# A hybrid retention and sliding-window layer on one core: the opening update of retention put into its first step, and the order of all engines planned with other numbers

## The chip, the core and the metric

The kernel runs on one core of one Trainium2 chip. The time is that of one execution on the device, in microseconds (us). Three runs of the kernel before took 667.78, 668.63 and 671.33 us; the median, 668.63 us, is the time before. A profiled execution leaves a trace with the start and duration of each instruction on the matmul engine (PE, with its weight loads shown apart as PEld), the vector engine (DVE), the scalar engine (ACT), POOL and the queue of SP, which issues the DMAs.

## The reference, cut to what matters

```python
h = rms_norm(x, norm_w)                       # (1, 2048, 1024)
proj = einsum('bsd,de->bse', h, w_in)         # 1024 -> 2816 columns
rq, rk, rv, rg, sq, sk, sv, sg = split(proj, offsets)
rq, rk = rotary(rq), rotary(rk)               # 4 heads of 64
ro = retention(rq, rk, rv)                    # chunks of 128 tokens, values of 128 a head
ro = group_norm_per_head(ro) * ret_norm_w * silu(rg)
so = sliding_window_attention(rms(sq), rms(sk), sv, sinks, rel_bias) * silu(sg)
out = x + concat(ro, so) @ w_out              # 1024 -> 1024
```

In retention each of 16 chunks has four parts: an update of the state (its keys against its values), scores (queries against keys, times a decay mask), a cross part (queries against the state of the chunks before) and an output part (scores against values).

## The kernel before

**Products.** The projections are made in four large products: the window's columns (W2, 512 wide), retention's queries, keys and first values (W1, 384), the gates (W3, 512) and the output (W4, 512). Each is a fast matrix product of seven smaller products over eight pairs of chunks, and each small product is 12 matmuls: four blocks of the inner dimension by three passes (high by high, high by low, low by high, written `acc<-w,x`). DVE and ACT split every operand into its high and low part and add the results up. The order on PE is W2, then W1, then W3, then W4.

**Other work on PE.** Between the small products stand the window's logits (`m<-ks,qT`, 64 matmuls for a pair of chunks, each of two passes in the trace), its values (`m<-pT,vn`, 72 for a pair), single transposes of keys (`m<-ident,kn`), transposes of gated retention outputs (`m<-ident,ro` or `m<-ident,go`, four for a chunk), and retention's steps. These use parts of the array (32 or 64 rows or columns) and not the whole, and each is one operation of the planner with many instructions.

**Retention's steps.** The loop at the end of `retention` makes one PE operation for each step from -1 to 8: the cross part of the pair of chunks before (`m<-state,qkT`), the update of the pair after (`m<-v,qk`), the scores of this pair (`m<-qkT`) and the outputs of the pair before (`m<-v,sT`). Each part takes 16 matmuls. Step -1 holds only the update of pair 0, in two banks of PSUM; step 0 holds the update of pair 1 and the scores of pair 0. Inside a step `mark`, two tiny copies on DVE, keeps the cross part and the outputs in order. After a step ACT moves the outputs out (`ro`), DVE takes their statistics (`st`), masks the scores (`sT`) and adds up the states (`state`).

**What sets the order.** Nothing runs in the order in which the code names it. `op` records each operation with a cost and a due time, and `Program.emit` plans them greedily: at each turn it takes the operation that can start first, and of those the one with the earliest due time. `SHIFT` moves the due times by label, `SHARE` limits how many buffers a use may hold, `AHEAD` and `AHEAD_OF` how far ahead of PE loads and splits may go. `WIN`, `RET` and `GATE` are the first due time and the distance of the chunks of the window, of retention and of the gates, counted in small products; `LEAD` says how early a gate must be ready. On PE a change between whole-array and partial-array matmuls is charged, and `LATER`, `CROWD`, `MOST` and `SOONER` gather such operations.

**Instruction blocks.** `emit` also counts PE's instructions (`many`, times `MORE` = 1.0125 for what is added later): a block border stands at `FIRST` = 193 and every `PIECE` = 256 after it, a block is taken to be asked for `ASKED` instructions ahead of its border and to take `LONG` us, and an operation that would come to a border sooner is planned later.

**Where results wait.** `HELD` lists results that stay in SBUF and are not stored and loaded again: sums of x for the products W1 and W3, retention's outputs (`ro`), the window's queries (`q`) and outputs (`so`), and gates. `TURNED` lists what is transposed through a store and a transposing DMA; what is not in it is transposed on PE. `EARLIER_Q`, `EARLIER_K` and `SCALED` set how early the queries and keys go on that way.

Of the kernel before, what the change touches and what calls it, by code (L numbers as in the profile page):

```python
# [39 lines left out]
P = 128  # L40
NCH = S // P
NP = NCH // 2
# [21 lines left out]
SHARE = {"x": 56, "raw": 221, "acc": 63, "wr": 28, "wh": 18, "att": 23, "ret": 40, "rin": 186, "gate": 29, "mix": 89, "norm": 17, "res": 29, "turned": 11, "vn": 3, "first": 5, "block": 3, "rest": 6}  # L64

AHEAD_OF = {"x": 5.5, "wh": 15.5}

AHEAD, SPARE, SPARED = 11.0, 4, ("raw", "wr")

# [25 lines left out]

PIECE, FIRST, ASKED, LONG, MORE = 256, 193, 320, 5.5, 1.0125  # L100

LATER, CROWD, MOST, SOONER = -3.75, 7.25, 41, -388.0
SETTLED, INSIDE = 0.8, 0.3


# [230 lines left out]

LOG = None  # L340

SHIFT = {"base": -3.5, "load xk": 0.5, "add s": 1, "load g": 3.75, "add t": -5.0, "silu": -1, "add res": -1.25, "square x": -2.5, "load phases": -0.25, "store so": -1.0, "decay": 0.5, "scale v": 1.25, "turn weights": -0.75, "no values": -0.5, "sink": -3.25, "hi w": 0.5, "load wr": 1.0, "load aq": -0.25, "qn": 0.25, "step": -0.5, "load akv": 0.25, "store r": -0.75, "store x": 1.5, "apart": 0.5, "sum so": 1.25, "load gp": -3.5, "copy s": -0.75, "sum x": 1.0, "load dec": 0.25, "store res": -0.75, "exp sink": 0.75, "store c": 0.25, "turn k": -1.5, "load vn": 0.75, "ro": -0.75, "turn by dma": -1.25, "load nw_sb": 0.5, "load go": 0.75, "ks": -1.25, "gate": -0.25, "kn": -0.5, "copy c": 0.75, "add r": -0.75, "scale w": 1.25, "rotary sum": -0.75, "factors": -0.5, "state": -0.25, "so": -1.25, "sum qk": -1.0, "load ": 0.25, "mixed": 0.75, "load snk": 0.25, "store ": -1.25, "rotary": 1, "more": 3.25, "bias": 1.25, "denominator": -0.75, "normalise": -1.25, "load wq": -0.25, "no keys": -1, "square qk": -1, "turn gated": -0.5, "load tri": -1, "exp": -1.25, "load bias": 0.25, "store s": -0.5, "logits": -1, "sum go": -1, "values": -0.5, "stats": 1.5}

TURN = (1.9635, 2.7, 1.35)


HELD = {"sums": ((3, 2), (3, 6), (3, 7), (5, 0), (5, 1), (5, 2), (5, 5), (6, 1), (6, 3), (6, 4), (6, 6)), "ro": (1, 2, 6, 10, 11, 13, 15), "q": (1, 3, 9, 12, 13), "gates": (), "so": (13,)}

TURNED = {"q": range(NCH), "qk": range(NCH), "gated": (3, 7, 14)}
EARLIER_Q, EARLIER_K = 5.5, 10.0
SCALED = (-25.0, 4.45)


def dve(n, two=False, lat=0.08):
# [24 lines left out]
def f32(n, count):  # L382
    t = count * (n / 600 + 0.01)
    return {"T": (t, t + 0.25, False)}
# [43 lines left out]
def layer(ctx, tc, xt, xfirst, xtok, nw, w_in, w_rn, qkw, sinks, biasg, rope, decays, dmask, gpow, w_out, out):  # L428
# [33 lines left out]
    def ps(share="rest", name="m"):  # L462
        return Buf("bank", None, F32, name, share)
# [60 lines left out]
    dec = fixed([P, 2, BASED, RH], "dec")  # L524
    factors = [fixed([P, NCH, RH], f"factors{i}") for i in range(2)]
# [178 lines left out]
    sums = {}  # L704
# [50 lines left out]
    turn = Buf(name="turn", ap=())  # L755
# [154 lines left out]
    def retention(at):  # L910
# [16 lines left out]
        for c in range(NCH):  # L927
            due = at(c)
            a, v = kb("a", "rin"), kb("v", "rin")
# [5 lines left out]
            if c % NP == 0:  # L935
                phases = kb("phases", "rin")
# [42 lines left out]
            else:  # L979

                def go(e, pt=pt, qk=qk):
# [6 lines left out]
                   label="qkT")  # L988
# [4 lines left out]
        norm = {}  # L993
# [28 lines left out]
        def update(c, pkv):  # L1022

            _, qk, _, v, v0, v1 = chunks[c]

            def go(e):
                for pr in range(2):
                    for i in range(2):
                        for b in range(2 if c < NCH - 1 else 1):
                            h, r, o = 2 * pr + i, halves[b], c % 2 * 256 + pr * P  # L1030
                            e.matmul(
                                pkv[b]()[halves[i], o : o + P], qk()[r, 256 + h * 64 : 256 + (h + 1) * 64],
                                v()[r, h * P : (h + 1) * P], start=True, stop=True,
                            )

            return go, [qk, v0, v1], [v]
# [48 lines left out]

            return go, [*sTs, v0, v1], [v]

        for step in range(-1, NP + 1):
            due = at(2 * step + 1)
            pair = lambda p: (2 * p, 2 * p + 1)  # L1090

            parts, writes, also, n, done = [], [], [], 0, None
            if step > 0:
                pros, begun, mark = [ps(), ps()], set(), sb("mark", [P, 2])

                def ordered(e, mark=mark, pros=pros):
                    for i in range(2):
                        V.tensor_copy(mark()[:, i : i + 1], pros[i]()[:, 256:257])

                writes += pros  # L1100
                parts += [cross(c, pros, ready[c], begun) for c in pair(step - 1)] + [(ordered, [], [mark])]
                n += 4
            if step < NP - 1:
                pkv = [ps(), ps()]
                writes += pkv
                parts += [update(c, pkv) for c in pair(step + 1)]
                n += 4
            if 0 <= step < NP:
                pss, sT = [ps(), ps()], sb("sT", [P, 512])
                writes += pss  # L1110
                also.append(sT)
                parts += [scores(c, pss) for c in pair(step)]
                n += 2.4
            if step > 0:
                parts += [outputs(c, pros, inside[0]) for c in pair(step - 1)]
                also.append(inside[1])
                n += 4

            def go(e, parts=parts):
                for part in parts:  # L1120
# [10 lines left out]
            if 0 <= step < NP:  # L1131
# [11 lines left out]
            if step < NP - 1:  # L1143
                for c in pair(step + 1):
# [477 lines left out]

WIN = (58.5, 4.0)
RET = (126.0, 2.25)
GATE = (138.5, 6.65)

LEAD = 14.0


_SHAPES = {
# [92 lines left out]
```

## Time and profile before

| | |
|---|---|
| median of three runs | 668.63 us (667.78 to 671.33) |
| the profiled execution | 672.41 us, of which 670.6 us from its first to its last instruction |
| instructions | 16293 |
| work on PE | 5960 matmuls and 5960 weight loads |
| mean granted PE clock | 0.997 |
| HBM | 96.79 MB read, 49.09 MB written |

All rows carry line L424, that of the helper that records each instruction, so operations are told apart by their tiles. A matmul of float32 operands runs in two passes and shows as two in the trace. In the rows of idle time, "issue" is time in which an engine waited for nothing that the profile shows.

### The profile page before, as it was taken

The numbers are of one execution on the slowest core, as the hardware profiler recorded it, in microseconds if no ns is written. First come the engines' busy times: TensorE is split into PE (matmuls) and PEld (weight loads), VectorE is DVE, ScalarE is ACT, GpSimd is POOL, SyncE is SP. The second block draws the span as 40 slices with busy tenths as digits, with TensorE's granted clock in tenths as the row PEclk, the third lists the DMA queues.
The fourth block names the chain that finished last, engine by engine and source line by source line (L and its number), as shares of the span: only waits on it lengthen the run. The fifth ranks groups of instructions, "written<-read, shape, count | busy, mean of one in ns | idle before, by whom it ended". The sixth has DMA issues, their size and how long they took to land.

```text
span 670.6 us, 16293 instructions
## 1 busy us (share of the span) xinstructions
PE 660.4 (98%) x5960; PEld 564.8 (84%) x5960; DVE 590.5 (88%) x1372; ACT 470.7 (70%) x1149; POOL 15.1 (2%) x39
## 2 busy tenths in 40 slices
PE   9999999999989999899999999999999999999998
PEld 7888888889979999899888888878888888888886
DVE  5999969778897998799999999979699999998762
ACT  6673897658689876596988989788999736344200
POOL 0000000023200000000000000000000000000000
PEclk9999999999989999999999999999999999999999
DMA  9965897879886978799999989898999894536222
GB/s 323 367 215 185 276 340 257 285 236 289 275 199 177 307 229 258 250 312 305 301 246 267 272 225 283 198 275 245 279 273 224 240 222 143 169 111 216 99 94 95
DMA packets 150688, 160.33 MB, mean 239 GB/s; under 512 B 64592, under 2 KB 92112, under 8 KB 150608
## 3 DMA queue, kind: packets, MB, share of 16 engines
q1 hardware_dynamic: 150464, 159.29, 80.6%
q8 instruction: 47, 0.77, 0.5%
q14 instruction: 33, 0.27, 0.2%
q10 hardware_dynamic: 144, 0.00, 0.0%
HBM read 96.79 MB, written 49.09 MB: 218 GB/s over the span
## 4 chain that ended last, share of the span: by engine, by line
PE 96%; DVE 2%; issue 1%; ACT 1%; DMA 0%; SPq 0%; ACTq 0%; DVEq 0%
PE acc L424 85%; PE m L424 11%; DVE st L424 0%; DMA v<-rq_dram 0%; ACT qk L424 0%; DVE t L424 0%; DVE x L424 0%; DVE r L424 0%; ACT apart L424 0%; DVE w L424 0%; ACT g L424 0%; DVE qk L424 0%; ACT w L424 0%; DVE mark L424 0%; DVE sT L424 0%
## 5 line engine op out<-in xcount | busy, mean ns | idle before, releaser
L424 PE MATMUL acc<-w,x 128*128 128x512 f32 (+1 forms) x2700 | 589.8, 378 | 2.3 <-issue 2.3
L424 PEld LDWEIGHTS acc<-w,x 128*128 128x128 f32 x2700 | 494.5, 189 | 86.1 <-issue 7.0
L424 DVE TENSOR_TENSOR x<-x 128x512 fp32r<-128x512 f32 (+2 forms) x220 | 143.2, 675 | 13.1 <-ACT x L424 11.2
L424 ACT ACTIVATE x<-x 128x512 fp32r<-128x512 f32 (+1 forms) x187 | 111.1, 619 | 25.9 <-PE acc L424 10.4
L424 DVE TENSOR_TENSOR w<-w 128x512 fp32r<-128x512 f32 (+3 forms) x96 | 60.5, 653 | 1.5 <-ACT w L424 1.5
L424 ACT ACTIVATE lg<-lg,nm 128x160 f32<-128x160 f32 x128 | 53.0, 418 | 6.2 <-DVE nm L424 6.1
L424 DVE TENSOR_TENSOR s<-acc,s 128x512 f32<-128x512 f32 (+1 forms) x64 | 41.6, 650 | 17.4 <-PE acc L424 17.0
L424 DVE SCALAR_TENSOR_TENSOR w<-w,nw_sb 128x512 fp32r<-128x512 f32 (+3 forms) x72 | 49.2, 706 | 1.7 <-ACT w L424 1.5
L424 ACT ACTIVATE w<-w 128x512 fp32r<-128x512 f32 (+1 forms) x72 | 41.4, 601 | 13.0 <-DVE w L424 5.8
L424 DVE CUSTOM_DVE_ANT_0 lg<-m,bias,nsnk 128x160 f32<-128x160 f32 x128 | 40.4, 375 | 3.6 <-PE m L424 3.6
L424 DVE TENSOR_TENSOR t<-acc,t 128x512 f32<-128x512 f32 (+2 forms) x33 | 21.1, 638 | 17.9 <-PE acc L424 17.5
L424 ACT ACTIVATE x<-go 128x512 fp32r<-128x512 f32 x31 | 19.2, 627 | 16.2 <-DVE x L424 5.4
L424 ACT ACTIVATE w<-w,nw_sb 128x512 fp32r<-128x512 f32 (+3 forms) x42 | 27.1, 678 | 4.0 <-DMA w<-in_w_in 2.3
L424 ACT ACTIVATE s<-acc 128x512 f32<-128x512 f32 (+1 forms) x32 | 18.1, 568 | 15.2 <-PE acc L424 14.9
L424 DVE STREAM_TRANSPOSE pT<-lg 128x640 f32<-128x640 f32 x32 | 26.0, 825 | 0.6 <-ACT lg L424 0.6
L424 DVE TENSOR_TENSOR r<-acc,t 128x512 f32<-128x512 f32 (+1 forms) x32 | 20.9, 652 | 5.9 <-PE acc L424 5.5
L424 ACT ACTIVATE qk<-qk,factors 128x64 f32<-128x64 f32 x64 | 17.0, 339 | 12.6 <-DVE mdif L424 7.0
L424 ACT ACTIVATE ro<-ro,nmu,rg 128x128 f32<-128x128 f32 x64 | 25.3, 482 | 0.3 <-DVE nmu L424 0.2
L424 ACT ACTIVATION_READ_ACCUMULATOR lg<-lg,nm 128x1 f32 x128 | 24.2, 189 | 0.0
L424 DVE TENSOR_TENSOR t<-acc,s 128x512 f32<-128x512 f32 (+1 forms) x32 | 20.7, 648 | 3.7 <-PE acc L424 2.8
L424 PE MATMUL m<-ks,qT 64*32 64x160 f32 x1024 | 20.1, 298 | 2.8 <-issue 2.8
L424 ACT ACTIVATE ro<-m 64x256 f32<-64x256 f32 (+2 forms) x55 | 22.1, 402 | 0.6
(140 smaller groups left out, 578.5 us busy)
## 6 DMA issues: line engine op xcount, KB each, us to landing
x<-in_xt SPq DMA_DIRECT2D x80, 256.0 KB, 4.7
planes_dram<-apart SPq DMA_DIRECT2D x51, 256.0 KB, 3.8
x<-s_dram SPq DMA_DIRECT2D x42, 256.0 KB, 4.2
w<-in_w_in SPq DMA_DIRECT2D x40, 256.0 KB, 5.3
xk<-in_xtok SPq DMA_DIRECT2D x32, 256.0 KB, 4.5
res<-in_xtok SPq DMA_DIRECT2D x32, 256.0 KB, 3.7
s_dram<-x SPq DMA_DIRECT2D x21, 256.0 KB, 3.9
w<-in_w_out SPq DMA_DIRECT2D x20, 256.0 KB, 4.5
```

The costliest lines, as they stand in the source:

```text
L424: return lambda *a, **k: self.order.put(op(*a, **k))
```

## The change

Retention's step -1 is gone. Step 0 now makes the updates of pair 0 and of pair 1, into four banks (two a pair), with the scores of pair 0. `many`, the planner's count of instructions, is 17 higher for a step. `TURNED` has four gated chunks (1, 8, 12, 14) in place of three (3, 7, 14). All other edits are numbers of the planner: shares, due times, distances, and what is held: seven sums in place of eleven, eight `ro` in place of seven, three `so` in place of one, one gate in place of none, and five `q` as before.

```diff
-SHARE = {"x": 56, "raw": 221, "acc": 63, "wr": 28, "wh": 18, "att": 23, "ret": 40, "rin": 186, "gate": 29, "mix": 89, ...
-AHEAD_OF = {"x": 5.5, "wh": 15.5}
-AHEAD, SPARE, SPARED = 11.0, 4, ("raw", "wr")
+SHARE = {"x": 24, "raw": 192, "acc": 88, "wr": 63, "wh": 56, "att": 56, "ret": 50, "rin": 279, "gate": 77, "mix": 93, ...
+AHEAD_OF = {"x": 8.0, "wh": 9.5}
+AHEAD, SPARE, SPARED = 24.5, 2, ("raw", "wr")
...
-PIECE, FIRST, ASKED, LONG, MORE = 256, 193, 320, 5.5, 1.0125
+PIECE, FIRST, ASKED, LONG, MORE = 256, 193, 300, 5.0, 1.0125
...
-LATER, CROWD, MOST, SOONER = -3.75, 7.25, 41, -388.0
+LATER, CROWD, MOST, SOONER = -2.0, 0.75, 35, -928.0
...
-HELD = {"sums": ((3, 2), (3, 6), (3, 7), (5, 0), (5, 1), (5, 2), (5, 5), (6, 1), (6, 3), (6, 4), (6, 6)), "ro": (1, 2, 6, 10, 11, 13, 15), "q": (1, 3, 9, 12, 13), "gates": (), "so": (13,)}
+HELD = {"sums": ((3, 2), (3, 5), (3, 6), (5, 2), (5, 7), (6, 2), (6, 5)), "ro": (0, 4, 5, 6, 7, 8, 12, 15), "q": (0, 5, 11, 13, 14), "gates": (3,), "so": (1, 12, 15)}
...
-TURNED = {"q": range(NCH), "qk": range(NCH), "gated": (3, 7, 14)}
-EARLIER_Q, EARLIER_K = 5.5, 10.0
-SCALED = (-25.0, 4.45)
+TURNED = {"q": range(NCH), "qk": range(NCH), "gated": (1, 8, 12, 14)}
+EARLIER_Q, EARLIER_K = 2.0, 6.5
+SCALED = (-30.5, 5.15)
...
-        for step in range(-1, NP + 1):
+        for step in range(NP + 1):
...
-            if step < NP - 1:
-                pkv = [ps(), ps()]
+            pkvs = {p: [ps(), ps()] for p in ((0, 1) if step == 0 else (step + 1,)) if p < NP}
+            for p, pkv in pkvs.items():
                 writes += pkv
-                parts += [update(c, pkv) for c in pair(step + 1)]
+                parts += [update(c, pkv) for c in pair(p)]
                 n += 4
...
-                f32(P, 0.935 * n), go, reads, writes, due + 0.4, "quarters", label="step", also=also, many=int(16 * n),
+                f32(P, 0.935 * n), go, reads, writes, due + 0.4, "quarters", label="step", also=also, many=int(16 * n) + 17,
...
-WIN = (58.5, 4.0)
-RET = (126.0, 2.25)
-GATE = (138.5, 6.65)
-LEAD = 14.0
+WIN = (56.5, 3.9)
+RET = (120.5, 1.45)
+GATE = (143.5, 4.5)
+LEAD = 15.5
```

How the order moves, at three places. Rows that follow each other and are alike are counted as one (x12).

On PE, the opening of retention, before, from the first update to step 0:

```order
L424 MATMUL acc<-w,x 128x512 x3
L424 MATMUL m<-v,qk 64x128 x16
L424 MATMUL acc<-w,x 128x512 x21
L424 MATMUL m<-ident,kn 128x128
L424 MATMUL acc<-w,x 128x512 x21
L424 MATMUL m<-ks,qT 32x160 x64
L424 MATMUL acc<-w,x 128x512 x42
L424 MATMUL m<-v,qk 64x128 x16
L424 MATMUL m<-qkT 64x64 x16
```

and now, with the step that follows:

```order
L424 MATMUL acc<-w,x 128x512 x33
L424 MATMUL m<-v,qk 64x128 x32
L424 MATMUL m<-qkT 64x64 x16
L424 MATMUL acc<-w,x 128x512 x51
L424 MATMUL m<-state,qkT 64x128 x12
L424 MATMUL m<-v,qk 64x128 x16
L424 MATMUL m<-qkT 64x64 x16
L424 MATMUL m<-v,sT 64x128 x16
L424 MATMUL acc<-w,x 128x512 x33
```

The visit with the first 16 updates is gone, and its matmuls stand in the next one.

On PE, in the window's part, before, one place at which values and logits stand close:

```order
L424 MATMUL m<-pT,vn 64x128 x32
L424 MATMUL m<-pT,vn 64x256 x8
L424 MATMUL m<-pT,vn 64x128 x32
L424 MATMUL m<-ident,kn 128x128
L424 MATMUL acc<-w,x 128x384 x18
L424 MATMUL m<-ks,qT 32x160 x64
L424 MATMUL acc<-w,x 128x384 x48
```

and now the closest place:

```order
L424 MATMUL m<-pT,vn 64x128 x32
L424 MATMUL m<-pT,vn 64x256 x8
L424 MATMUL m<-pT,vn 64x128 x32
L424 MATMUL acc<-w,x 128x384 x18
L424 MATMUL m<-ks,qT 32x160 x64
L424 MATMUL acc<-w,x 128x384 x21
L424 MATMUL m<-pT,vn 64x128 x32
L424 MATMUL m<-pT,vn 64x256 x8
L424 MATMUL m<-pT,vn 64x128 x32
L424 MATMUL acc<-w,x 128x384 x48
```

A second set of values now follows the logits after 21 products, where 48 stood before.

On PE, the last two steps of retention, before:

```order
L424 MATMUL acc<-w,x 128x512 x42
L424 MATMUL m<-state,qkT 64x128 x16
L424 MATMUL m<-qkT 64x64 x16
L424 MATMUL m<-v,sT 64x128 x16
L424 MATMUL acc<-w,x 128x512 x36
L424 MATMUL m<-ident,go 128x128 x4
L424 MATMUL acc<-w,x 128x512 x24
L424 MATMUL m<-state,qkT 64x128 x16
L424 MATMUL m<-v,sT 64x128 x16
L424 MATMUL m<-ident,ro 128x128 x4
```

and now:

```order
L424 MATMUL acc<-w,x 128x512 x21
L424 MATMUL m<-state,qkT 64x128 x16
L424 MATMUL m<-qkT 64x64 x16
L424 MATMUL m<-v,sT 64x128 x16
L424 MATMUL acc<-w,x 128x512 x9
L424 MATMUL m<-state,qkT 64x128 x16
L424 MATMUL m<-v,sT 64x128 x16
L424 MATMUL acc<-w,x 128x512 x45
L424 MATMUL m<-ident,ro 128x128 x4
```

The steps stand closer: between the last two are 9 products in place of 60, and between the steps ahead of them 51, 33, 27, 36, 27, 48 and 21. The transposes of gated outputs, which stood between the steps and far into W4, now all come after the last step and before W4's first product.

More of the change, by code (lines that the diff above doesn't have):

```diff
@@ L62 @@
 SMALL, COUNTS = 3, {"ms": 1, "rxt": 1, "rqk0t": 1, "rqk1t": 1, "state": 10, "sT": 2}
-SHARE = {"x": 56, "raw": 221, "acc": 63, "wr": 28, "wh": 18, "att": 23, "ret": 40, "rin": 186, "gate": 29, "mix": 89, "norm": 17, "res": 29, "turned": 11, "vn": 3, "first": 5, "block": 3, "rest": 6}
-AHEAD_OF = {"x": 5.5, "wh": 15.5}
-AHEAD, SPARE, SPARED = 11.0, 4, ("raw", "wr")
+SHARE = {"x": 24, "raw": 192, "acc": 88, "wr": 63, "wh": 56, "att": 56, "ret": 50, "rin": 279, "gate": 77, "mix": 93, "norm": 17, "res": 24, "turned": 22, "vn": 3, "first": 5, "block": 3, "rest": 6}
+AHEAD_OF = {"x": 8.0, "wh": 9.5}
+AHEAD, SPARE, SPARED = 24.5, 2, ("raw", "wr")
 STEPS = ((1, 2), (6,), (5,), (7, 4), (3,))
@@ L340 @@
 LOG = None
-SHIFT = {"base": -3.5, "load xk": 0.5, "add s": 1, "load g": 3.75, "add t": -5.0, "silu": -1, "add res": -1.25, "square x": -2.5, "load phases": -0.25, "store so": -1.0, "decay": 0.5, "scale v": 1.25, "turn weights": -0.75, "no values": -0.5, "sink": -3.25, "hi w": 0.5, "load wr": 1.0, "load aq": -0.25, "qn": 0.25, "step": -0.5, "load akv": 0.25, "store r": -0.75, "store x": 1.5, "apart": 0.5, "sum so": 1.25, "load gp": -3.5, "copy s": -0.75, "sum x": 1.0, "load dec": 0.25, "store res": -0.75, "exp sink": 0.75, "store c": 0.25, "turn k": -1.5, "load vn": 0.75, "ro": -0.75, "turn by dma": -1.25, "load nw_sb": 0.5, "load go": 0.75, "ks": -1.25, "gate": -0.25, "kn": -0.5, "copy c": 0.75, "add r": -0.75, "scale w": 1.25, "rotary sum": -0.75, "factors": -0.5, "state": -0.25, "so": -1.25, "sum qk": -1.0, "load ": 0.25, "mixed": 0.75, "load snk": 0.25, "store ": -1.25, "rotary": 1, "more": 3.25, "bias": 1.25, "denominator": -0.75, "normalise": -1.25, "load wq": -0.25, "no keys": -1, "square qk": -1, "turn gated": -0.5, "load tri": -1, "exp": -1.25, "load bias": 0.25, "store s": -0.5, "logits": -1, "sum go": -1, "values": -0.5, "stats": 1.5}
+SHIFT = {"square qk": -2.5, "load g": 3.0, "silu": -3.75, "hi w": 1.0, "no values": -2.0, "decay": -2.0, "store ro": 7.5, "copy s": -4.25, "exp sink": 7.0, "denominator": 4.25, "qn": 1.0, "turn k": -8.0, "load ": 2.25, "lo w": 0.5, "store ": -8.0, "sum w": -1.0, "load vn": 2.5, "step": -6.5, "sink": -1.25, "load w": 0.25, "turn weights": -7.0, "scale v": -0.25, "more": 4.0, "no keys": -4.5, "group norm": 1.5, "add res": 9.0, "sum x": 0.25, "gate": -1.25, "load go": -4.5, "rotary sum": -0.25, "load k4": -2.0, "load bias": 4.25, "normalise": 5.5, "store res": 8.75, "so": 4.75, "sum go": 3.75, "base": -5.5, "load aq": -8.75, "store s": 1.5, "store t": -6.5, "store x": -2.25, "load xk": -0.75, "kn": 1.25, "load akv": -0.75, "sum so": -1.5, "state": -4.0, "values": -5.5, "load dec": 3.5, "copy c": 3.0, "add s": -1.0, "rotary": -0.75, "load phases": -1.5, "stats": 2.0, "add t": -0.25, "ks": -2.0, "store apart": -0.5, "logits": -0.5, "lo x": 0.25, "load gp": 0.25, "load res": 2.0, "square x": 2.0, "load nw_sb": 3.75, "add r": -1.75, "bias": -2.75, "turn by dma": 0.25, "mixed": -1.0, "scale w": 3.75, "store r": 1.5, "exp": -2.5, "sum ro": 0.5, "turn gated": 0.5, "load wr": -1.25, "store c": 0.25, "load snk": 1.25, "load tri": -0.75, "store so": -0.5, "scale k": -0.5, "load wq": -1}
@@ L1102, in retention @@
                 n += 4
-            if step < NP - 1:
-                pkv = [ps(), ps()]
+            pkvs = {p: [ps(), ps()] for p in ((0, 1) if step == 0 else (step + 1,)) if p < NP}
+            for p, pkv in pkvs.items():
                 writes += pkv
-                parts += [update(c, pkv) for c in pair(step + 1)]
+                parts += [update(c, pkv) for c in pair(p)]
                 n += 4
-            if 0 <= step < NP:
+            if step < NP:
                 pss, sT = [ps(), ps()], sb("sT", [P, 512])
@@ L1130, in retention @@
                     evacuate(c, pros, due)
-            if 0 <= step < NP:
+            if step < NP:
                 sTs = [Part(sT, lambda t, i=i: t[:, i * 256 : (i + 1) * 256]) for i in range(2)]
@@ L1142, in retention @@
                 inside = (sTs, sT)
-            if step < NP - 1:
-                for c in pair(step + 1):
+            for p, pkv in pkvs.items():
+                for c in pair(p):
                     states = [state]
```

## The prediction

> **What bounds the kernel now.** I read the page's share of engines first, then PE's waits, then the stretches around those waits, then PE's timeline and the DMA queues there.
>
> ```profile
> span 670.6 us, 16293 instructions
> PE 660.4 (98%) x5960; PEld 564.8 (84%) x5960; DVE 590.5 (88%) x1372; ACT 470.7 (70%) x1149; POOL 15.1 (2%) x39
> PE m L424 <- issue: 2.8, 2, 2.2
> PE acc L424 <- issue: 2.3, 1, 2.3
> PE m L424 <- DVE none L424: 1.2, 1, 1.2
> PE m L424 <- DVE sT L424: 0.3, 1, 0.3
> PE m L424 <- DVE mark L424: 0.3, 1, 0.3
> 194.00:198.00 4.00, 1.81 (x89) 1.23 (x75) 3.87 (x17) 4.00 (x10) 0.00 (x0) 0.97 1.22 204
> 198.00:208.00 10.00, 10.00 (x50) 9.96 (x51) 6.29 (x26) 6.22 (x29) 0.00 (x0) 0.84 0.82 226
> ```
>
> PE is the bound: it is busy 98% of the span, and all its waits together are 6.9 us. Only 0.6 us of them are for another engine's work once the kernel runs; 5.1 us (2.8 + 2.3) are "issue", where no semaphore was late. After the first of these the granted clock (third number from the right) is 0.97 for 4 us and 0.84 for 10 us, a loss of 4 x 0.03 + 10 x 0.16 = 1.7 us. So 7.4 us can be won from waits and clock (5.1 + 1.7 + 0.6), and the rest is matmul work that the change hardly touches. The largest gain is therefore near 1.1%, while there is no such limit on the other side.
>
> What are the issue waits? Three stretches from the start to each wait count PE's matmuls before it:
>
> ```profile
> 0.00:195.05 195.05, 193.87 (x1235) 164.85 (x1236) 165.87 (x330) 139.53 (x327) 15.07 (x39) 1.00 0.83 273
> 0.00:222.75 222.75, 219.37 (x1614) 188.95 (x1614) 189.80 (x398) 160.77 (x391) 15.07 (x39) 0.99 0.83 266
> 0.00:268.85 268.85, 264.86 (x2373) 231.81 (x2373) 230.69 (x526) 196.15 (x513) 15.07 (x39) 0.99 0.85 264
> q8 instruction: 47, 0.77, 0.5%
> ```
>
> Two instructions a matmul (with its weight load), times the planner's 1.0125, give 2501, 3268 and 4805. Less 193 that is 9.02, 12.01 and 18.02 times 256: each wait stands on a block border. The last row is the page's queue of instruction fetches: 47 packets of 0.77 MB / 47 = 16 KB, and 5960 x 2 x 1.0125 / 256 = 47 blocks. PE waits for its own instructions. The third wait on the timeline and in the queues:
>
> ```profile
> 260.00 2.54 PE L424 MATMUL m<-pT,vn 32*64 32x128 f32 x144
> 262.47 1.84 PE L424 MATMUL acc<-w,x 128*128 128x384 f32 x9
> ...
> 264.17 1.81 PE L424 MATMUL acc<-w,x 128*128 128x384 f32 x9
> 265.91 2.43 PE L424 MATMUL m<-ks,qT 64*32 64x160 f32 x128
> 268.27 0.62 PE L424 MATMUL acc<-w,x 128*128 128x384 f32 x2
> 271.16 6.71 PE L424 MATMUL acc<-w,x 128*128 128x384 f32 x37 [2.27 <-issue]
> q8 instruction: 1, 0.02, 36.2%
> q1 hardware_dynamic: 1619, 1.40, 65.5%
> q8 instruction: 1, 0.02, 39.1%
> ```
>
> The three queue rows are of the stretches 260.8 to 261.1, 262.0 to 268.6 (no instruction packet at all) and 268.65 to 268.8 us. One fetch starts at 260.8 to 261.1, the next only at 268.65, as PE already stands, and PE goes on at 271.16, about 10.2 us after the first. Values (288 instructions in 2.47 us) and logits (256 in 2.36 us) eat a block each; 18 products between them are too few to cover a fetch.
>
> A rule of the Trainium skill speaks against this reading: "Runtime: NRT & Kernel Launch", Instruction fetch mechanics, says that blocks of 16 KiB (256 instructions) are fetched while the one before runs, and that the cost of a border is mostly hidden. The block's size agrees with the 16 KB above; that it is hidden does not, at these three borders of 47. It is the third rival below.
>
> **The change part by part.**
>
> *The joined update.* One visit of PE to partial-array work goes, the 16 matmuls of the order (32 in the trace) stay:
>
> ```profile
> 331.42 0.97 PE L424 MATMUL acc<-w,x 128*128 128x512 f32 x3
> 332.32 1.10 PE L424 MATMUL m<-v,qk 64*64 64x128 f32 x32
> 333.35 5.06 PE L424 MATMUL acc<-w,x 128*128 128x512 f32 x21
> 378.48 1.05 PE L424 MATMUL m<-v,qk 64*64 64x128 f32 x32
> 379.35 0.64 PE L424 MATMUL m<-qkT 64*64 64x64 f32 x32
> 421.67 0.44 PE m L424 x4
> 525.17 34.73 PE acc L424 x153
> ```
>
> From 331.42 to 333.35 are 1.93 us. Three products are 0.68 (34.73 / 153 = 0.227 each) and 32 update matmuls inside a step are 379.35 - 378.48 = 0.87, so the visit cost 1.93 - 0.68 - 0.87 = 0.38 us. That goes: **-0.4**. Four banks and two for scores make six, what any middle step holds, and 51 products (11.6 us) follow before the next step asks for banks; if that cover fails, products wait for the eight `state` adds.
>
> *A fourth gated chunk turned by DMA.* Four transposes less on PE, 0.44 us by the row of x4: **-0.4**. It adds a copy on ACT (70% busy), a store and a transposing DMA.
>
> *What is held.* Four sums less are four stores and eight loads more (W1 and W3 both read them); one `ro`, two `so` and one gate more held save eight. With the turned chunk, SP issues six transfers more, 1.5 MB of 160 MB. They hide behind queues that carry 239 GB/s on average with no row of PE waiting for a DMA; uncovered they would be 1.5 MB / 239 GB/s = 6.4 us, shared by all that wait.
>
> *The new order and the blocks.* I walk PE's new order with the durations above (values 2.47, logits 2.36, a product 0.174 or 0.227, a change of array about 0.2), counting instructions as for the waits, and take the time for two blocks, since the waits came where two in a row were short. In the order before this gives, below 10.6 us: 7.7 (the first wait, 2.19), 7.7 (the third, 2.27), and 10.0, 10.5, 10.5, 10.5, of which one waited 0.61 and three not at all. The wait is thus about 9.9 us less the span. The new order has 9.1, 9.1, 7.9, 8.1 and 10.3. The 7.9 is the triple values, 18 products, logits, 21 products, values; the 8.1 overlaps it by a block, so that a wait of 2.0 in the one lengthens the other to 10.1. The waits become 0.8 + 0.8 + 2.0 + 0 + 0.3 = 3.9 in place of 5.1: **-1.2**. Bounds: 0, if blocks come as early as at most borders, and 7.2 by counting places alone (three spacings of 21 products or less in place of two, 2.2 each, and 0.6). I take 3.9, since it follows the borders.
>
> *The clock.* Of two waits of 2.2 us, one was followed by a low clock and one not. With one such wait left I take half of 1.7: **-0.85** (bounds -1.7 and +1.7). The Trainium skill ("TensorE: Matmul & The Clock Gate", What's actually happening) has the clock fall after an idle window of about 3.4 us that runs free of the kernel. A wait of 2.19 us did it here. By that page no wait of 2 us would, and the sum would be 0.85 lower.
>
> *PE's waits for DVE.* 0.6 us now; the steps move closer together, so these may move too: **-0.3**, between -0.6 and what the second rival gives.
>
> Sum: -0.4 - 0.4 - 1.2 - 0.85 - 0.3 = -3.15 us, so the profiled execution goes from 672.41 to 669.3. Of the 672.41, 1.8 lie outside the span and stay. The execution lies 3.8 us above the median of the runs, and 672.41 - 7.4 = 665.0 is its time with no wait and full clock, so the median loses only 668.63 - 665.0 = 3.6 of the 7.4. If the median moves by the whole sum it becomes 665.5; if its waits and clock shrink in that proportion (0.49 x 2.35 = 1.15, and 0.8 for work), 666.7. I predict **666.0 us**, 0.4% faster, with 664 to 668.5 as this case's own range.
>
> **The rivals.**
>
> *Blocks in time.* The planner now asks 300 instructions ahead and counts 17 more for a step, so that its borders may fall where the chip's do. The new order has no span as short as 7.7. If all waits and the low clock go, 665.0 - 0.8 = 664.2 us. Against it: the 7.9 and 8.1 in one place.
>
> *Retention too dense for DVE.* Slower.
>
> ```profile
> 407.02 1.10 PE L424 MATMUL m<-state,qkT 64*64 64x128 f32 x32
> 410.27 11.40 PE L424 MATMUL acc<-w,x 128*128 128x512 f32 x48
> 400.00:420.00 20.00, 20.00 (x202) 16.43 (x201) 19.80 (x55) 19.26 (x47) 0.00 (x0) 1.00 0.94 271
> L424 DVE TENSOR_TENSOR state<-m,state 128x256 f32<-128x256 f32 x30 | 12.4, 413 | 0.0
> L424 DVE BATCH_NORM_STATS2 st<-ro 128x6 f32<-128x128 f32 x64 | 13.8, 276 | 0.0
> L424 DVE TENSOR_TENSOR sT<-m,tri 128x256 f32<-128x256 f32 x16 | 6.6, 411 | 0.0
> L424 DVE TENSOR_TENSOR s<-acc,s 128x512 f32<-128x512 f32 x48 | 32.9, 685 | 9.1 <-PE acc L424 8.8
> L424 DVE TENSOR_TENSOR x<-x 128x512 fp32r<-128x512 f32 x180 | 120.6, 685 | 12.9 <-ACT x L424 11.2 <-DMA rq_dram<-s 0.8 <-DMA aq_dram<-t 0.5
> ```
>
> A step takes 410.27 - 407.02 = 3.25 us of PE, and 48 products 10.9: 14.1 us a round. On DVE a step needs four `state` adds (1.65), eight statistics (13.8 / 64 each, 1.7), two masks (0.8), and each small product one add and one split (1.36): 4.2 + 4 x 1.36 = 9.6 us. That leaves DVE 4.5 us a round for gates and weights, and it was busy 19.80 of 20 us. With 27 products the round is 3.25 + 6.1 = 9.4 us and DVE's part 4.2 + 3.1 = 7.3: 2.1 us are left. If the 2.4 us that go are not done elsewhere, PE waits as much in each of the four rounds of 27 to 36 products: +9.6, less the 3.15 above, 668.63 + 6.5 = 675. It decides once DVE is more than the two free banks behind, 2 x 12 x 0.227 = 5.4 us. For it: between the last two steps stand 9 products (2.0 us), and one of the two waits for DVE before was for `mark`, the copy inside a step. Against it: DVE idles 80 us of 670, and its work that is due later can stand behind.
>
> *The waits are chance.* Of 47 borders 44 were passed without a wait, among them three spans of 10.0 to 10.5 us. If a wait depends on what the data queues carry at that moment and not on the span, new places get their like, and only the 0.8 of work goes: 667.8. For it: of the four spans near 10 us one waited and three did not. Against it: both shortest spans waited. The skill's rule of hidden fetches, above, would also leave the order without effect.
>
> **How the numbers follow.** A measurement here tells about 0.5% from no change: below 665.3 is faster, above 672.0 slower. Forecast 0.52 (0.20 of it below 665.3, 0.30 between, 0.02 above); blocks in time 0.18, faster; DVE 0.22, slower; waits by chance 0.08, between. Together faster 0.38, same 0.38, slower 0.24. The range, 663 to 674, takes in the first rival and most of the second's way up to 675.
>
> **What would show it.** Right: PE still at 98% or 99%, issue waits of 3 to 5 us in all, the longest at the values that follow logits after 21 products, and the update of four chunks as one run of 64 matmuls. Wrong: waits of PE for DVE or ACT above 2 us in sum among the steps (second rival); issue waits at places that are no border (third); more than 6 us of issue waits, which would break the rule for two blocks.

## The result, and the profile after

The changed kernel takes 675.66 us (median of five runs, 674.37 to 677.67); the kernel before, run beside it, 669.72 (667.78 to 672.20). The measured ratio is 1.0081, 95% interval 1.0055 to 1.0107 (the two medians alone give 1.0089): the change makes the kernel slower by 0.8%. The profiled execution is the median run. The profiled execution of the kernel before, 672.41, lies above the highest of its runs, so the two profiles differ by 3.3 us where the medians differ by 5.9.

The page of the kernel after, its first two rows, and what PE waited for (microseconds in all, times, longest):

```profile
span 673.9 us, 16316 instructions
PE 660.3 (98%) x5956; PEld 564.5 (84%) x5956; DVE 593.0 (88%) x1369; ACT 476.4 (71%) x1152; POOL 15.8 (2%) x39
PE m L424 <- issue: 6.9, 3, 3.0
PE m L424 <- DVE none L424: 1.2, 1, 1.2
PE acc L424 <- ACT w L424: 1.1, 1, 1.1
PE acc L424 <- ACT x L424: 0.9, 1, 0.9
PE m L424 <- DVE mark L424: 0.3, 1, 0.3
```

PE's busy time is what it was (660.3 after 660.4). What grew are its waits: issue from 5.1 to 6.9, and two rows that the kernel before did not have, 1.1 for the first weight and 0.9 for a block of x. The retention steps, which stand closer now, wait 0.3 us in all (`mark`); the 0.9 for a block of x comes between two of them.

The stretches that end where the three issue waits begin, with PE's matmuls in brackets behind its busy time, and the one around the first wait (third number from the right: granted clock):

```profile
0.00:220.37 220.37, 217.97 (x1613) 187.29 (x1614) 190.77 (x421) 164.57 (x407) 15.79 (x39) 1.00 0.89 287
0.00:250.35 250.35, 244.92 (x2118) 212.47 (x2118) 216.16 (x492) 183.95 (x476) 15.79 (x39) 0.99 0.87 276
0.00:300.36 300.36, 293.84 (x3002) 258.67 (x3002) 263.20 (x648) 228.77 (x626) 15.79 (x39) 0.99 0.89 273
220.00:240.00 20.00, 16.97 (x287) 15.65 (x278) 15.53 (x45) 13.04 (x49) 0.00 (x0) 0.91 0.77 180
```

By the count of the prediction (2 x 1.0125 instructions a matmul, less 193) the waits stand at 12.0, 16.0 and 23.0 times 256: on block borders again, but on others. The clock loses 20 x 0.09 = 1.8 us behind the first, about as much as before (1.7).

The start, on the timeline: ACT's copy of the first weight, before,

```profile
3.66 0.72 ACT L424 ACTIVATE w<-w,nw_sb 128x512 fp32r<-128x512 f32 x1 [1.00 <-DMA w<-in_w_in]
```

and after, with PE's first products:

```profile
5.34 0.72 ACT L424 ACTIVATE w<-w,nw_sb 128x512 fp32r<-128x512 f32 x1 [0.23 <-DMA w<-in_w_in]
6.12 0.73 PE L424 MATMUL acc<-w,x 128*128 128x512 f32 x2 [1.15 <-ACT w L424]
```

The planner's new numbers put two loads of x ahead of the first weight on SP. That weight is copied 1.7 us later, and the products, which on the chain followed the warming matmuls at 4.97 us before, start at 6.12, with 1.15 us of wait. Not all of that lasts in these two executions: the first products of the kernel before are slow (its second to fifth come 0.43 us apart, those of the changed kernel 0.23), and by the trace the 600th product starts at 141.50 us before and at 142.02 after, 0.5 us apart.

The profiles' 3.3 us are so: issue +1.8, start +0.5, the block of x +0.9, DVE -0.3, clock behind the waits 0, work +0.4 (the rest).

### The profile page after: what moved, and what is told of

It is laid out like the page before. It is cut to its first block, busy times and chain, and to the rows that moved or that the text cites. A ratio compares the mean times of both kernels' runs of the same rounds, so it can differ in the third digit from the quotient of the medians.

```text
span 673.9 us, 16316 instructions
## 1 busy us (share of the span) xinstructions
PE 660.3 (98%) x5956; PEld 564.5 (84%) x5956; DVE 593.0 (88%) x1369; ACT 476.4 (71%) x1152; POOL 15.8 (2%) x39
## 4 chain that ended last, share of the span: by engine, by line
PE 87%; ACT 3%; DMA 3%; DVE 3%; issue 2%; SPq 1%; ACTq 0%; DVEq 0%
PE acc L424 78%; PE m L424 9%; DVE w L424 1%; DMA w<-in_w_in 1%; DMA planes_dram<-apart 1%; ACT apart L424 1%; ACT qk L424 1%; ACT lg L424 1%; SPq L424 1%; DVE x L424 0%; DMA a<-rq_dram 0%; DMA x<-in_xt 0%; DMA v<-aq_dram 0%; DVE pT L424 0%; DVE t L424 0%
## 5 line engine op out<-in xcount | busy, mean ns | idle before, releaser
L424 ACT ACTIVATE w<-w,nw_sb 128x512 fp32r<-128x512 f32 (+3 forms) x44 | 29.0, 694 | 5.4 <-PE acc L424 2.8
L424 PE MATMUL m<-pT,vn 32*64 32x128 f32 (+1 forms) x1152 | 21.4, 286 | 6.9 <-issue 6.9
L424 PEld LDWEIGHTS m<-pT,vn 32*64 32x64 f32 x1152 | 18.6, 130 | 9.7 <-issue 9.7
L424 ACT ACTIVATE x<-go 128x512 fp32r<-128x512 f32 x27 | 16.6, 627 | 12.6 <-PE acc L424 3.7
```

The source lines that it names most:

```text
L424: return lambda *a, **k: self.order.put(op(*a, **k))
```

## The experiments

Each kernel was timed against the kernel before on the same chip: 671.47 us for the first four, 670.11 for the next four, 671.02 for the last three. Ratios to it are therefore what is compared across groups.

My theory was that the place of the block borders in the program sets the waits, and that the start adds up to 1.15 us. Where a border falls can be moved without touching the order: a number of instructions is added on PE ahead of the first border that matters, and every later border falls on other work. 256 more put each border back on the same work.

### The kernel before, 160 instructions more at the start

```diff
-        for _ in range(WARM):
+        for _ in range(1):
             e.matmul(pw()[:, 0:256], none()[:, 0:P], none()[:, 0:256], start=True, stop=True)
+        for _ in range(43):
+            e.matmul(pw()[0:32, 0:32], none()[0:32, 0:32], none()[0:32, 0:32], start=True, stop=True)
```

> The kernel before, its order unchanged; of the four warming matmuls ahead of the first product three are left out and 43 tiny ones put in (160 instructions more), so that every border of PE's instruction blocks falls 160 instructions earlier in the order. Theory (PE waits for its own blocks where two of them are asked for within about 3.5 us): no border then has two requests so close, the issue waits among the window's logits and values (5.1 us in the profile before) and the low clock after them go: issue waits under 1.5 us, time 665 (663.5 to 667), ratio to before 0.990 to 0.996. Rival (the waits are chance or belong to the operations and not to the borders): issue waits of 3 to 7 us as before, time 668 to 672. Second rival (retention too dense for DVE) says nothing here.

Measured: 668.69 us (667.34 to 670.14), ratio 0.9962 (0.9947 to 0.9977), span 665.5. All that PE waited for:

```profile
PE m L424 <- DVE none L424: 1.2, 1, 1.2
PE m L424 <- DVE sT L424: 0.3, 1, 0.3
PE m L424 <- DVE mark L424: 0.3, 1, 0.3
```

There is no issue wait left, though the kernel does more and its products start 2.4 us later on the timeline (7.06 us, 4.70 in the kernel before).

### The changed kernel with 112 and with 256

The same edit with 31 and with 67 tiny matmuls.

> The changed kernel, its order unchanged, with 112 instructions more ahead of the first product (three warming matmuls less, 31 tiny ones more). Theory of the borders: the three issue waits of the changed kernel (3.0, 1.1 and 2.7 us) and the low clock go: issue waits under 1.5 us, time 667 (665.5 to 669), that is 8 to 9 us under the changed kernel and about 0.4% under before. Rival (chance, or the operations): issue waits near 7 us, 674 to 677.5. Rival (retention too dense): the loss sits among the steps, so the time stays above 673.

> The changed kernel with 256 instructions more ahead of the first product, a whole block (three warming matmuls less, 67 tiny ones more): the borders fall on the same places of the order as in the changed kernel. Theory of the borders: issue waits of 6 to 8 us at the same three sets of values, time 675.7 (674 to 678), plus up to 1.5 us if the tiny matmuls delay the first product. Rival (the tiny matmuls themselves or any other order of fetches help): like the kernel with 112 more, 665.5 to 669.

Measured: with 112, 672.99 us (672.05 to 677.58), ratio 1.0043 (1.0023 to 1.0064). The three old waits are gone, but four smaller ones stand at new borders (1.26, 1.67, 0.55 and 0.44 us), 3.9 us where I had expected less than 1.5. The tiny matmuls also leave the first products slow: the 600th starts at 143.31 us, 1.3 later than in the changed kernel. The two together make up most of the 6 us by which the 667 expected was missed. With 256, 679.36 us (677.45 to 682.80), ratio 1.0135 (1.0109 to 1.0161). On the chain of waits (start, us, what) of the kernel with 256 are the same three places:

```profile
222.82 2.20 PE m L424 x119
225.02 1.96 issue
...
251.89 2.02 PE m L424 x108
253.91 1.36 issue
...
302.18 2.15 PE m L424 x114
304.33 2.04 issue
```

In the changed kernel the waits also come behind 119, 108 and 114 matmuls of those sets of values. Places follow the count modulo 256; lengths vary by a microsecond from one execution to the next (5.4 us in all here, where I had expected 6 to 8). This control is slow by its start: the first product begins at 9.62 us and the 600th at 147.03, 5.0 later than in the changed kernel. Two of its waits, of 1.96 and 2.04 us, were followed by 3.4 us of half clock, one more than there.

### The first weight load first, on SP alone

```diff
...
-            o.go(engines[e])
+            if e == "Q" and turn is not None:
+                turn.append(o)
+                if len(turn) == 3:
+                    for x in (turn[2], turn[0], turn[1]):
+                        x.go(engines[e])
+                    turn = None
+            else:
+                o.go(engines[e])
```

> The changed kernel with one thing moved: the first weight load is issued ahead of the first two loads of x, as in the kernel before (there weight, x, weight, x). Everything else keeps its order. Theory of the start: the first product waits for the first weights (first product at 6.1 us, 5.0 before); it starts at 5.0 to 5.4 us, and the time falls by 0.8 to 1.2 us against the changed kernel, to 674.6, with the issue waits as they were. Rival (the start is hidden by later slack): first product earlier, the time the same within 0.3 us.

Measured: 676.87 us (674.70 to 680.32), ratio 1.0099 (1.0071 to 1.0126), a miss: the first product starts at 6.78 us, no earlier. The weight's load went first, but ACT's own order has copies of x ahead of the weight's, and those began at 4.45 us in place of 3.70, since their loads now came later. The start is an order on two engines.

### The start of the kernel before, on every engine

The first 60 operations of the planner are held and handed out in the order that the kernel before gives the same 60.

```diff
+OPEN = [1, 0, 11, 1429, 2, 3, 379, 14, 384, 17,
...
-            o.go(engines[e])
+            if done < len(OPEN):
+                held[o.n] = o, engines[e]
+                for n in OPEN if done + 1 == len(OPEN) else ():
+                    held[n][0].go(held[n][1])
+            else:
+                o.go(engines[e])
```

> The changed kernel with its first 60 operations handed out in the order of the kernel before (first weight load ahead of the first x load on SP, its copy first on ACT); all later work in the changed order. Theory: the first product starts at 4.9 us and not at 6.1, everything behind it 1.15 us earlier, the three issue waits of 6.9 us unchanged: 674.5 us where the changed kernel has 675.7. Rival (the start is made good later, since DVE or a load sets the pace): no change, 675.7.

Measured: 673.43 us (670.18 to 677.20), ratio 1.0053 (1.0027 to 1.0080), span 673.3; the first products on the chain of the changed kernel and of this one, and PE's issue waits:

```profile
6.12 158.36 PE acc L424 x705
...
4.97 158.20 PE acc L430 x705
...
PE m L430 <- issue: 7.1, 4, 2.8
PE acc L430 <- issue: 0.3, 1, 0.3
```

On the chain the first product starts at 4.97 us, as before the change. The span fell by only 0.6 in this execution since its issue waits are 7.4 in place of 6.9; the ratio fell by 0.0028, or 1.9 us. The two intervals overlap, so of the time alone the start's part is not shown to better than that. Its 1.15 us at the first product are, and they last: the same 705 products end at 163.17 us here and at 164.48 in the changed kernel, 1.3 later.

### A shift that does not delay the start: 160 and 256 in the kernel before

80 or 128 of the first stage's 512-wide matmuls become two of 256 each, as here; the sums and the order stay.

```diff
+    halved = [0]
...
-                    e.matmul(
-                        acc()[:, :n], a()[:, cols], b()[:, :n], start=(not goes_on and k == i == 0),
-                        stop=(k == 3 and i == 2), skip_group_check=goes_on,
-                    )
+                    many = 2 if n == 512 and halved[0] < 80 and (goes_on or k + i) else 1
+                    halved[0] += many - 1
+                    for h in range(many):
+                        at = slice(h * n // many, (h + 1) * n // many)
+                        e.matmul(
+                            acc()[:, at], a()[:, cols], b()[:, at], start=(not goes_on and k == i == 0),
+                            stop=(k == 3 and i == 2 and h == many - 1), skip_group_check=goes_on,
+                        )
```

> The kernel before, with 80 of the first products' 512-wide matmuls split into two of 256: 160 more instructions on PE ahead of the first block border that mattered, the same sums, every engine's order unchanged, no delay of the start. Theory (the instruction waits hang on where the borders fall): as with the 160 instructions of tiny matmuls, no issue wait of more than 0.3 us and no half clock after the start; the split costs 80 x 0.02 = 1.6 us by the rows of the 256-wide and the 512-wide products (125 and 231 ns each), the first product starts at 5.0 us as before; profiled span 670.6 - 5.1 - 1.7 + 1.6 = 665.4 or less, median about 666.5. Rival (the tiny matmuls helped only because they delayed the first products by 2 us and let the loads get ahead): the waits of 5 us stay, span 672.

> Control for the one above: 128 matmuls split, 256 instructions, one whole block, so every border falls on the same work as in the kernel before. Theory: the issue waits stay at the values and logits where they were (2.2, 0.6 and 2.3 us in its profile, give or take 1), and the split costs 128 x 0.02 = 2.6 us: 671 to 675, 5 us or more behind the kernel with 160. Rival (more instructions early help whatever their number): no waits here either, about 668.

Measured: with 160, 666.03 us (665.03 to 666.81), ratio 0.9935 (0.9909 to 0.9960). The span is 664.3. All of PE's waits, and the whole and the halved products:

```profile
PE m L424 <- DVE none L424: 1.2, 1, 1.2
PE m L424 <- DVE mark L424: 0.5, 1, 0.5
PE m L424 <- DVE sT L424: 0.3, 1, 0.3
L424 PE MATMUL acc<-w,x 128*128 128x512 f32 x1924 | 445.5, 391 | 0.1
L424 PE MATMUL acc<-w,x 128*128 128x256 f32 x184 | 22.4, 283 | 0.0
```

A whole product is 445.5 / 1924 = 0.2315 us of PE, two halves are 2 x 22.4 / 184 = 0.2435, 12 ns more, so 80 splits cost about 1 us. For that, 5.1 us of waits and 1.7 of clock are gone: 664.3 is 670.6 - 6.8 + 1.0 within 0.5.

With 256, 671.62 us (670.68 to 674.83), ratio 1.0034 (1.0012 to 1.0055). 48 splits more cost about 0.6 us, and the time is 5.6 us longer, because two of the three waits of the kernel before are back at their places (the third, 0.6 there, is 0.07 here):

```profile
194.29 2.06 PE m L424 x110
196.35 1.40 issue
...
264.47 2.36 PE m L424 x128
266.82 2.75 issue
```

Of 160 and 256 instructions early, only the number that is no whole block helps. The rival (a later start helps the loads) is out.

### The changed kernel with the old start and 136

> The changed kernel with the start of the kernel before and 136 more PE instructions early (68 matmuls split). Theory: the three waits at the old places go; new ones of 0 to 3 us in sum may come at other borders; split +1.2, start -1.15: profiled span 673.9 - 6.9 - 1.7 + 1.2 - 1.15 + 1.5 = 667, median 668 (666.5 to 670). If the waits are all that keeps the changed kernel behind, it stands level with the shifted kernel before to within its own waits and the 0.9 us wait for ACT. Rival (the changed order is slower in the work itself): over 672 with waits under 2 us.

Measured: 666.77 us (665.19 to 668.35), ratio 0.9941 (0.9922 to 0.9960), span 665.5. The timeline at the changed kernel's first wait, after (the rows left out are 6 products and a transpose of keys),

```profile
210.41 2.43 PE L424 MATMUL m<-ks,qT 64*32 64x160 f32 x128
...
214.26 3.91 PE L424 MATMUL acc<-w,x 128*128 128x384 f32 x21
218.10 2.27 PE L424 MATMUL m<-pT,vn 32*64 32x128 f32 x124
223.40 0.83 PE L424 MATMUL m<-pT,vn 32*64 32x128 f32 x20 [3.03 <-issue]
```

and in this kernel the products and values at the same place, with two rows of its waits (besides `none` 1.2 and `mark` 0.3, as after):

```profile
213.94 3.88 PE L430 MATMUL acc<-w,x 128*128 128x384 f32 x21
217.75 2.53 PE L430 MATMUL m<-pT,vn 32*64 32x128 f32 x144
...
PE m L430 <- issue: 1.5, 1, 1.5
PE acc L430 <- ACT x L430: 0.8, 1, 0.8
```

Logits, 6 and 21 products and values stand as close as they did, and PE walks through. As far as two single executions tell, the order of the change is no slower in itself: without its waits (1.5 and 0.8, `none` 1.2, `mark` 0.3) and 68 splits (0.8) it is 665.5 - 4.6 = 660.9, and the shifted kernel before, less 1.2, 0.8 and 1.0, is 664.3 - 3.0 = 661.3.

### Waits forecast ahead: 240 in the kernel before

120 splits. From the traces so far I had the rule that the expectation states, with a block asked for some 45 instructions ahead of the border before it. The rule is a fit to the fetches' starts, not something that a row states: no row tells when a block is asked for.

> A place forecast ahead: the kernel before with 240 early instructions (120 matmuls split), order unchanged. Theory (a block is asked for some 45 instructions ahead of the border before it; when two are asked for within 3.6 us, the second's transfer starts 6.5 to 8.5 us behind the first's, and PE goes on 2.3 us later): the longest issue wait is at the 10th border after the start of the blocks, at about 196 to 200 us, 3 to 5 us long; a second of 0.3 to 2.3 at about 222 to 226; none at 242 and 268, where the kernel before has its second and third; sum 3.3 to 7.3 us, a half clock of 3.4 us after the long one: span 664.3 + 0.3 + 5.3 + 1.7 = 671.6, median 673. Rival (waits belong to the first values after the logits, wherever the borders lie): waits of 2 us at three places as in the kernel with 256, median 671.5.

Measured: 673.65 us (671.37 to 675.41), ratio 1.0048 (1.0028 to 1.0068). The chain:

```profile
193.72 2.30 PE m L424 x118
196.02 3.41 issue
...
223.97 2.29 PE m L424 x117
226.27 0.47 issue
```

The long wait is at 196.0 us, 1362 matmuls in, which is 10.0 blocks, and of 3.4 us; the second is at 226.3 and of 0.5. The expectation has the second wait of the kernel before at 242 us; it is at 222.8, so this second one came near an old place and tells little. Against the control with 256 every border falls on work 16 instructions later, and that small step made the first wait longer (1.40 to 3.41), as the rule had it; the rival would have left three waits of 2 us. The last one (2.75 at 266.8 there) shrank to 0.8 us, six products on, where the rule had none: a partial miss. Nor was it forecast that the clock stays at half for 6.8 us behind the first in place of 3.4. The first wait stands inside logits here and in the kernel before, in the changed kernel all three inside values: no kind of work owns them.

### The joined update alone, and the numbers without it

First: the code of the change with all numbers of the kernel before, planned anew (two of the lines are below), and 160 by splitting. Second: the numbers of the change with the step ahead of the first put back, the old start and 136.

```diff
-PIECE, FIRST, ASKED, LONG, MORE = 256, 193, 300, 5.0, 1.0125
+PIECE, FIRST, ASKED, LONG, MORE = 256, 193, 320, 5.5, 1.0125
...
-RET = (120.5, 1.45)
+RET = (126.0, 2.25)
```

> The joined update alone: the code of the change, planned with all the numbers of the kernel before, and 160 more early instructions (80 matmuls split), the shift that took every issue wait out of the kernel before. To be held against that shifted kernel (span 664.3, median 666.0). Theory (the joined update saves one visit, about 0.4 us, and adds no wait): no issue wait over 0.5 us, span 663.9, median 665.6. Rival (64 update matmuls in a row leave the cast and the decay late: DVE waits in the first steps): DVE waits of 2 us or more, median 667.5 or more.

> The changed kernel's planning numbers without the joined update (the step ahead of the first is back), with the start of the kernel before and 136 early instructions, against the same with the join (span 665.5 with 1.5 us of issue waits, median 666.8). Theory: the visit comes back, +0.4 us; borders fall as there up to the update and again behind the first step, so issue waits of 1 to 2.5 us: span 665.9, median 667.2. Rival (the join was a loss in this order): 666.0 or less.

Measured, the first: 664.99 us (664.38 to 665.63), ratio 0.9919 (0.9900 to 0.9938), span 663.8. All of PE's waits:

```profile
PE m L424 <- DVE none L424: 1.2, 1, 1.2
PE acc L424 <- DVE nm L424: 0.5, 1, 0.5
PE m L424 <- DVE mark L424: 0.3, 1, 0.3
PE m L424 <- DVE sT L424: 0.2, 1, 0.2
```

The span is 0.5 us below that of the shifted kernel without the join, and behind the start no wait of PE is over 0.5; by the ratios alone the two cannot be told apart (their intervals overlap), and single executions differ by more than 0.5 us. It is the fastest version here and beats both kernels.

The second: 678.18 us (676.32 to 679.80), ratio 1.0118 (1.0096 to 1.0139), a miss. Its order holds one wait of 6.8 us for a block of x:

```profile
PE acc L430 <- ACT x L430: 7.9, 3, 6.8
```

at 570 us, far behind the update: ACT's copy of that block waits 5.62 us for DVE, which works without a gap from 567 us on. Behind the wait the granted clock is 0.51 from 575 to 582 us. So the run says nothing of the join. It shows that these numbers did not serve the program with the step put back.

## Why the prediction failed, point by point

The forecast was 666.0 us and the result 675.66, on the other side of the kernel before. In the profiles the sum was to be 669.3.

- **What bounds the kernel** held: PE, 98%, with issue waits at block borders and the clock as what can be won. The shift of 160 wins it (0.9935), which is the first rival's end, "blocks in time"; the change itself did not bring it about.
- **The step that failed: "the new order and the blocks", -1.2.** It took the time for two blocks and made the wait 9.9 us less that span. Measured +1.8, 3.0 off. At the five borders with spans of 9.1, 9.1, 7.9, 8.1 and 10.3 it put 0.8, 0.8, 2.0, 0 and 0.3 us; the waits were 0, 3.0, 0, 2.7 and 1.1. Counted in the trace after, without the waits, these spans are 8.1, 9.3, 10.1, 8.2 and 10.5 us. So the walk had two of them wrong, by 1 and by 2 us, and the rule fails on the right ones too: 9.9 less the span would be 1.8, 0.6, 0, 1.7 and 0. The closest place (logits, 21 products, values) had its wait as said, 2.7 for 2.0; the longest, 3.0, came behind logits and 27 products, where the text had 0.8. The bound of 7.2 by counting places, which was set aside, lies nearest to the 6.9 in size alone.

  What the runs showed instead: a wait hangs on where the border falls in the work and on when that block's own fetch comes, and no size follows from the span. The same runs of short matmuls, shifted by 160 instructions in the kernel before, cost nothing (no two blocks take less than 11 us there); shifted by 136 in the changed kernel, two blocks of 8.7 us pass without a wait and two of 12.3 end in its wait of 1.5. Each of the thirty issue waits of 0.25 us or more in the thirteen traces stands within 0.03 block of a border, and PE goes on 2.2 to 2.8 us after the start of the last instruction fetch before that. That the fetch is late because two blocks are asked for close together is a reading, and not shown. The instruction queue (rows of its packets, where a stretch has any) shows this at the wait of 3.0 us, in stretches from 212.7 to 213.4, from 213.5 to 220.9 (no instruction packet) and from 220.95 to 221.7 us:

```profile
q8 instruction: 1, 0.02, 10.0%
...
q1 hardware_dynamic: 1195, 2.09, 88.1%
...
q8 instruction: 1, 0.02, 8.4%
```

  Some 8 us pass between the starts of the two fetches, PE stands from 220.37, the second starts at about 221.0, and PE goes on at 223.40. The prediction named more than 6 us of issue waits as what would break its rule; 6.9 came.
- **The clock, -0.85:** 0. One wait of the three was again followed by half clock, for 3.4 us.
- **The start, not in the sum:** +1.15 of wait, 1.3 by the run with the old start, 0.5 between the two profiles. The text walked the new order from the logits on and never looked at the first loads, which the same numbers had moved. The orders of SP and ACT held it.
- **A wait for ACT in retention, not in the sum:** +0.9, at 376 us. On the chain (start, us, what) a load of v from its store ends at 374.96, and ACT does `ro`, `apart`, `s` and `x` one behind the other:

```profile
372.09 2.87 DMA v<-aq_dram
374.96 0.38 ACT ro L424
```

  Which of the numbers put it there was not tried.
- **The joined update, -0.4,** was right, as the trace after shows on PE:

```profile
352.04 1.98 PE L424 MATMUL m<-v,qk 64*64 64x128 f32 x64
353.84 0.64 PE L424 MATMUL m<-qkT 64*64 64x64 f32 x32
```

  The updates take 353.84 - 352.04 = 1.80 us in one visit, where the two before took 1.93 - 0.68 = 1.25 and 0.87: 0.3 saved. The fourth gated chunk (-0.4) was not tried alone. PE's work without waits and splits is about 0.4 lower in the changed order between the two shifted kernels, and 0.4 higher between the two profiles above, where the two terms together were to give 0.8 less; single executions do not tell it better. **PE's waits for DVE, -0.3,** were right.
- **From profile to median, -3.3.** I took the excess of the one profiled execution of the kernel before over its runs along to the changed kernel. Its profiled execution is its median. Lengths of border waits vary between runs, so an excess that is made of them belongs to one execution.
- **The rivals.** "Retention too dense for DVE" named 675 us, and the time came, but not for its reason: 1.2 us of waits among the steps (0.3 for DVE, 0.9 for ACT), under the 2 that were named as its sign. "The waits are chance" is out: with 256 in place of 160 instructions the kernel before loses 5.6 us, and with 240 the first wait grew and the last shrank, the one as forecast and the other less than forecast. The rule of the Trainium skill that the prediction weighed ("Runtime: NRT & Kernel Launch", Instruction fetch mechanics: a border's cost is mostly hidden) holds for most borders; 3 of 47 here cost 6.9 us.

Of the 6.4 us between the sum and the profiled 675.66, issue waits are 3.0, the start 0.5, the block of x 0.9, the clock 0.85, and work the rest, 1.1.

## What to carry to other kernels

Where PE is the bound and runs of short matmuls eat a block of 256 instructions in 2 to 3 us, look for waits without a releaser, count the instructions up to each, and see whether they fall on multiples of 256. If they do, add cheap instructions early and measure more than one number of them: 160 cost about 1 us here and won 0.65%, where the new plan of the whole order lost 0.8%, but 240 made the kernel slower. A control with 256 tells the cause from the rest. And when a table of planning numbers changes, walk the first microseconds of the load queue and of the engine behind it first: the first weight's copy, 1.7 us later, put 1.15 us of wait on PE, which is busy for 98% of the span.

## What was unexpected in the hardware

- A fetch of 16 KB of instructions takes about 1 us in the queue (10.0% of 0.7 us times 16 engines is 1.1), and yet at the thirty waits the fetch that was waited for started 5.6 to 10.0 us after the one before it (212.8 and 221.0 in the changed kernel, 189.7 and 197.0 in the kernel with 240). Elsewhere two start some 3.5 us apart without a wait (244.6 and 248.1 in the kernel before). Why the one is so late is open.
- Half clock does not follow the length of a wait alone. 2.73 us in the changed kernel and 2.75 in the kernel before with 256 had none, 1.96 in the changed kernel with 256 and 2.19 in the kernel before had 3.4 us of it, and the wait of 3.41 us with 240 had 6.8. In the traces' records of the clock, full clock lasts a whole number of 3.413 us between two changes: 191.15 us (56 of them) in the kernel before, 218.45 (64) in the changed kernel, 215.04 (63) in it with 256. That fits a window that runs free of the kernel, as the Trainium skill ("TensorE: Matmul & The Clock Gate", What's actually happening) has it with about 3.4 us, though by that page no wait shorter than a window would do it, and 1.96 us did.
- Splitting a 512-wide product into two of 256, with a second weight load, costs PE only 12 ns.
